# Modulation vectors of a two-layer diffusion transformer: two chunks of columns to a PSUM bank, turned by transposes and added up by VectorE

## The chip, the cores and the metric

The kernel runs on one core of a Trainium2 chip. The time is what the device takes for one launch, in microseconds (us); the numbers of the kernel before come from three runs and one profiled execution. Engines are named as in the profile: PE (matrix products; PEld is its weight load), DVE (VectorE), ACT (ScalarE), POOL (GpSimd) and SP (here only a queue of DMA issues). PEclk is the clock that PE was granted, as a share of full speed.

## The reference

Everything is fp32. Two layers work on 512 tokens and 256 context tokens of width 1024. For each layer two vectors, `c` for the tokens and `c_ctx` for the context, give six modulation vectors of 1024 each:

```python
mod = silu(c) @ mod_w[l] + mod_b[l]          # 6 x 1024 columns, and the same for c_ctx
sh1, sc1, g1, sh2, sc2, g2 = split(mod, 6)
h = rmsnorm(x, ln1) * (1 + sc1) + sh1
x = x + g1 * (mixer(h) @ w_out)
h = rmsnorm(x, ln2) * (1 + sc2) + sh2
x = x + g2 * moe(h)
```

The mixer of layer 0 is dense attention (8 heads on 2 key heads) beside a convolution module; that of layer 1 is attention in a window, with the context and a sink, beside a pooling mixer. `moe` routes each token to 2 experts of 32.

## The kernel before

**Modulation.** `mod_w` comes in chunks of 512 columns, 12 a layer, four pages of 512 KB each (`load`, L126 to 131). `silu_c` holds silu(c) and silu(c_ctx) as two columns of a block of 32, the other 30 zero. `gemv` (L183 to 202) multiplies a chunk in eight products: four column groups of PE take a row block each, so a bank of PSUM has four partial sums in partitions 0, 32, 64 and 96 (and the next ones, for c_ctx), and a second round adds to them (L189). DVE copies the bank (L193). `finish`, which is called later, turns rows into columns and adds the four partial sums in one go: four products with the selection matrix `s2` (L198), each 128 columns of rows against 128x2. DVE adds the bias `mod_bT` from PSUM into `modT` (L199). PE executes an fp32 product as several records, so the trace shows 16 records for the eight products and 8 for the four selections. `gemv_first` (L204 to 222) does the same for the first four chunks of layer 0, in which a chunk holds 256 columns of the shift and 256 of the scale; it lies between the norms of the first tokens. Two more chunks are computed between the projections (`mixer_ab_in`).

**Who uses the columns.** `mod_rows` (L233 to 241) transposes eight column blocks, copies them (`grow`) and stores them to DRAM as a row, from where `row_bcast` (L256) reads it into all partitions: g1, A2 and B2 in the output projection. `router_bias` (L245 to 253) takes the second norm's shift through the router.

**Layer 0's attention** (`mixer_ab_att`) works on 24 units, a pair of heads and a tile of 128 queries each; three are in flight. In each step i PE does the scores of unit i (L482), the transposes of unit i-1's probabilities (L522) and the values of unit i-2 (L537); DVE takes the maxima (L493) and sums, ACT the exponentials (L500) and the copies of transposes (L530) and outputs (L450). `extra(i)` is called at the end of a step, `between(i)` in its middle; they carry the other work, among it taps of the convolution on DVE and POOL (L749, L760). Chunks 6 to 11 of layer 0 and 0 to 3 of layer 1 are computed in `extra` of i = 0, 2 ... 18, and each is finished in the next step. The stores of rows follow chunk 9.

**Layer 1's attention** (`mixer_cd_att`) has 16 units of the same kind. The remaining eight chunks of layer 1 are computed in i = 0 to 7; the weights w_out of the output projection are loaded in i = 4 and 5 and split into a rounded part (ACT, L290, `high`) and a rest (DVE, L295, `low`) one page a step in i = 6 to 13, the rest always in the next step's `between`. `low` gives the page's place back.

**Places and order.** All weights lie in a list of places of 4 KB a partition. A new tile takes the first place of the list, and its load or write waits till the last user of that place is done. The experts' loads (`ahead`, L1326 to 1335) are issued by SP as far as there are places in the list. Each engine keeps the program's order, but for PE, DVE and POOL in two stretches (layer 0's output projection and layer 1's attention), in which the compiler puts first what it holds to be ready. SP issues in the program's order within a stretch: at the start of layer 1's output projection these are 14 loads of experts' pages and then the load of `g1b`, the first gate in all partitions, which `OutProj` multiplies with the products of w_out (L626, L634), before X is updated (L635) and transposed for the second norm (L645).

```python
            if 0 <= n < len(jobs):
                fin.append(gemv(*jobs[n], mods.pop(0)))
                if todo:
                    mods.append(load(a["mod_w"][1, todo.pop(0)]))
                if n in (4, 5):
                    raw.append(load(a["w_out"][1, n - 4]))
```

Of the kernel before, what the change touches and what calls it, by code (L numbers as in the profile page):

```python
# [7 lines left out]
F32 = mybir.dt.float32  # L8
# [4 lines left out]
OP = mybir.AluOpType  # L13
# [26 lines left out]
# engines that do not keep the program's order, by region: 3 is the first layer's output projection, 6 the second's attention  # L40
FREE = {3: [PE, mybir.EngineType.DVE, POOL], 6: [PE, mybir.EngineType.DVE, POOL]}
# pages of the experts' first weights that a layer loads ahead: before the gate, and then at three points of its start
G1 = 3
FIRST = ((11, 0, 2), (7, 3, 2))
# pages beside the lasting ones that a layer's experts have: from the output projection on, and from the experts on
NT = (9, 11)
NS = (9, 3)
# chunks of the second layer's modulation: the tiles at which two are loaded, and how many the attention begins with
M1 = (4, 5)
M2 = 2  # L50
# the row block of the output projection after which the pages that were free before it are taken
# [17 lines left out]
def hybrid_dit_kernel(ctx: ExitStack, tc: tile.TileContext, a, out):  # L69
# [7 lines left out]
    def by_hand(r):  # L77
        """All engines but those given keep the program's order; those take what is ready first."""
        engines = set(ENGINES) - set(FREE.get(r, ()))
        if engines != held[-1]:  # L80
            held.append(engines)
            sched.close()
            sched.enter_context(tc.manual_schedule(engines=engines))
# [13 lines left out]
    class Pages:  # L97
        """Places of 4 KB a partition for weights and other data, each held by one tile after another: what is rounded
        for TensorE's one-pass products and what is not are tiles of their own."""
# [26 lines left out]
    def load(src, n=4, pools=None, queue=nc.sync):  # L126
        """The first n pages of a chunk of weights"""
# [33 lines left out]
    silu_c = keep.tile([128, KT, 32], F32, name="silu_c")  # L161
    modT = keep.tile([128, 2, 48, 2], F32, name="modT")

    def warm(func):
        """Has ScalarE load the function's table ahead of its use"""
# [15 lines left out]
    roomy = []  # L181

    def gemv(l, ch, w):  # L183
        """Products of a chunk of 512 columns; four column groups of the array take a row block each."""
        ps = sm("mps")
        for i in range(2):
            for g in range(4):
                k = 4 * i + g
                nc.tensor.matmul(ps[g * 32:(g + 1) * 32, :], silu_c[:, k, :], w[k // 2][:, k % 2 * 512:(k % 2 + 1) * 512],  # L189
                                 start=(i == 0), stop=(i == 1))  # L190
        pages.done(w)
# [3 lines left out]
        def finish():  # L195
            pt = sm("mpt")
            for b in range(4):
                nc.tensor.matmul(pt[:, 2 * b:2 * b + 2], rows[:, b * 128:(b + 1) * 128], C("s2"), start=True, stop=True)  # L198
            nc.vector.tensor_tensor(modT[:, l, ch * 4:ch * 4 + 4, :], pt[:, 0:8].rearrange("p (b r) -> p b r", r=2),  # L199
                                    mbT[:, l, ch * 4:ch * 4 + 4, None].to_broadcast([128, 4, 2]), OP.add)  # L200
        return finish

    def gemv_first(n, w):
        """The shift and the scale of a pair of row blocks in layer 0's first norm"""  # L204
        ps = sm("mps")
        for c in range(2):
            for i in range(2):
                for g in range(4):
                    nc.tensor.matmul(ps[g * 32:(g + 1) * 32, c * 256:(c + 1) * 256], silu_c[:, 4 * i + g, :],
# [5 lines left out]
        def finish():  # L215
            pt = sm("mpt")
            for b in range(4):
                nc.tensor.matmul(pt[:, 2 * b:2 * b + 2], rows[:, b * 128:(b + 1) * 128], C("s2"), start=True, stop=True)
            dst, b = (m[:, 0, 0:16].rearrange("p (c k) r -> p c k r", c=2)[:, :, 2 * n:2 * n + 2] for m in (modT, mbT[:, :, :, None]))
            nc.vector.tensor_tensor(dst, pt[:, 0:8].rearrange("p (c k r) -> p c k r", c=2, r=2),  # L220
# [1948 lines left out]
```

## Time and profile before

| | |
|---|---|
| runs | 1768.14, 1769.58 and 1769.0 us, median 1769.0 |
| profiled execution | 1769.0 us, the span of its profile |
| instructions | 24713 |
| PE busy | 1567.2 us, 89%; mean granted clock 0.966 |
| DVE busy | 913.2 us, 52% |
| ACT, POOL busy | 528.4 us (30%), 427.4 us (24%) |
| DMA | 519.03 MB, mean 293 GB/s |
| stages | start to 58 us, projections of layer 0 to 187, its attention to 331, its experts to about 990, layer 1's attention 1069 to 1180, its output projection to 1220, its experts to the end |

A row of the timeline gives the start, the duration, the engine, the line of the kernel, the output and inputs by the program's names and the shapes; equal instructions in a row are put together with their count, and their duration is from the first one's start to the last one's end. In brackets stands how long the engine was idle before, and whose end released it. The queue of an engine's DMA issues is named with a q (SPq).

### The profile page before, as it was taken

What the parts mean: (1) busy time and instruction counts of PE and PEld (TensorE: products, weight loads), DVE (VectorE), ACT (ScalarE), POOL (GpSimd) and SP (SyncE); (2) the same over time, 40 slices, a digit from 0 to 9 for tenths busy, and PEclk for the clock granted to TensorE, in tenths of its full rate; (3) what the DMA queues carried; (4) which work ended last, traced back from release to release, by engine and by line L of the source; (5) the groups of instructions that cost most, each with busy time, mean ns of one, the idle gap of its engine ahead of it and who ended that gap; (6) DMA issues with size and microseconds to landing.
All of it is one profiled execution on the core that took longest, in us unless ns stands there. A gap on an engine that the chain in (4) does not pass through costs nothing. (4 is left out here: it accounts for less than half of the span.)

```text
span 1769.0 us, 24713 instructions
## 1 busy us (share of the span) xinstructions
PE 1567.2 (89%) x8732; PEld 866.9 (49%) x8732; DVE 913.2 (52%) x1747; ACT 528.4 (30%) x1036; POOL 427.4 (24%) x347
## 2 busy tenths in 40 slices
PE   5979689997899999998986789989799999989997
PEld 4867457885333333332321676677334344343442
DVE  3897889788333232322333656656534445344454
ACT  3422468733111111111112434663312122121221
POOL 1535556132112112211111223201121121111110
PEclk9999799999999999999999899999799999999999
DMA  9121743447999999999998338145699999999992
GB/s 368 58 83 66 292 155 122 164 148 278 354 396 397 388 390 386 391 394 389 392 400 332 123 108 319 58 180 188 257 408 408 408 408 406 408 406 406 405 407 91
DMA packets 151597, 519.03 MB, mean 293 GB/s; under 512 B 22445, under 2 KB 23181, under 8 KB 151437
## 3 DMA queue, kind: packets, MB, share of 16 engines
q1 hardware_dynamic: 134300, 479.67, 69.2%
q0 software_dynamic: 11520, 16.81, 3.7%
q10 hardware_dynamic: 5616, 20.45, 3.0%
q8 instruction: 97, 1.59, 0.4%
q14 instruction: 64, 0.52, 0.1%
HBM read 510.49 MB, written 21.02 MB: 300 GB/s over the span
## 5 line engine op out<-in xcount | busy, mean ns | idle before, releaser
L1476 PE MATMUL gu<-w,xt 128*64 128x512 f32 x2304 | 516.7, 597 | 21.1 <-DMA w<-in_ex_dram 11.9
L1476 PEld LDWEIGHTS gu<-w,xt 128*64 128x64 f32 x2304 | 171.5, 137 | 326.6 <-issue 247.6
L1500 PE MATMUL yy<-w,ht 128*64 128x512 f32 x1152 | 264.8, 601 | 14.2 <-PEq L1296 5.9
L1482 DVE TENSOR_TENSOR hh<-hh,gu 128x512 f32<-128x512 f32 x64 | 44.1, 688 | 451.6 <-ACT hh L1481 451.6
L1481 ACT ACTIVATE hh<-gu 128x512 f32<-128x512 f32 x64 | 38.3, 598 | 566.2 <-PEq L1296 416.2
L1500 PEld LDWEIGHTS yy<-w,ht 128*64 128x64 f32 x1152 | 81.4, 137 | 172.4 <-issue 133.7
L1379 POOL DMA_INDIRECT xD<-ys,sidx x40 | 70.6, 1765 | 317.8 <-DVE ys L1375 315.3
L1409 POOL TENSOR_TENSOR lo<-ys,hi 64x1024 fp32r<-64x1024 f32 x29 | 68.2, 2351 | 325.0 <-ACTq L1296 325.0
L749 DVE SCALAR_TENSOR_TENSOR acc<-glu,convp,acc 128x784 f32<-128x784 f32 x76 | 97.9, 1288 | 1.6
L760 POOL TENSOR_TENSOR part<-part,prod 128x784 f32<-128x784 f32 x40 | 84.7, 2118 | 43.2 <-ACT prod L759 42.2
L1375 DVE TENSOR_TENSOR ys<-yy,ys 128x512 f32<-128x512 f32 x64 | 44.3, 692 | 97.8 <-PEq L1296 53.4
L1408 ACT ACTIVATE hi<-ys 64x1024 fp32r<-64x1024 f32 (+1 forms) x35 | 34.4, 983 | 193.1 <-DVE ys L1386 108.8
L1352 POOL DMA_INDIRECT Xg<-hD,gidx x40 | 42.6, 1066 | 188.9 <-PE xtp L1460 179.7
L264 POOL TENSOR_TENSOR rs<-ms,mhalf 128x1 f32<-128x1 f32 (+2 forms) x40 | 41.5, 1038 | 170.8 <-DVE ms L262 170.3
L1390 DVE TENSOR_TENSOR X<-X,cmb 128x512 f32<-128x512 f32 x126 | 77.0, 683 | 1.6 <-PE cmb L1426 1.1
L1426 PE MATMUL cmb<-hi,oh 128*128 128x512 f32 x128 | 58.0, 453 | 22.2 <-DVE oh L1413 20.5
L1460 PEld LDWEIGHTS xtp<-cst,Xg 128*128 128x128 f32 x512 | 58.0, 146 | 34.6 <-PEq L1296 18.6
L1460 PE MATMUL xtp<-cst,Xg 128*128 128x128 f32 x512 | 64.8, 282 | 9.1 <-PEq L1296 9.1
L522 PE MATMUL ptp<-cst,P 128*128 128x128 f32 x368 | 53.3, 284 | 18.7 <-POOL P L510 10.5
L1494 DVE COPY ht<-htp 128x512 f32<-128x512 f32 x64 | 43.8, 684 | 50.0 <-PE htp L1489 50.0
L695 PE MATMUL qps<-wh,hi 128*128 128x256 f32 (+1 forms) x176 | 61.4, 349 | 8.0 <-DVE hi L1819 2.4
L687 DVE TENSOR_SCALAR xt<-xtp,A,modT 128x128 f32<-128x128 f32 x128 | 49.6, 410 | 35.7 <-ACT xt L689 34.6
(310 smaller groups left out, 2633.9 us busy)
## 6 DMA issues: line engine op xcount, KB each, us to landing
w<-in_ex_dram SPq DMA_DIRECT2D x751, 512.0 KB
w<-in_mod_w_dram SPq DMA_DIRECT2D x96, 512.0 KB
w<-in_ex_dram ACTq DMA_DIRECT2D x17, 512.0 KB
w<-in_w_out_dram SPq DMA_DIRECT2D x16, 512.0 KB
w<-in_w_in_ab_dram SPq DMA_DIRECT2D x14, 512.0 KB
hD<-x ACTq DMA_DIRECT2D x8, 512.0 KB
xD<-X ACTq DMA_DIRECT2D x6, 512.0 KB
w<-in_w_in_cd_dram ACTq DMA_DIRECT2D x6, 512.0 KB
```

The lines of the kernel that those rows point to most:

```text
L522: nc.tensor.transpose(ps[:, (c - c0) * 128:(c - c0 + 1) * 128], u["P"][c // nk][:, c % nk * 128:(c % nk + 1) * 128], ident)
L687: nc.vector.tensor_scalar(dst[:, k, :], src, g, b, op0=OP.mult, op1=OP.add)
L695: nc.tensor.matmul(ps[:, o:o + n], h(x, k, tk), w(p, k, 0, n), start=(k == 0 and c == 0), stop=(k == KT - 1 and c == 2))
L749: nc.vector.scalar_tensor_tensor(acc, glu[:, ct, i:i + CW], w(i), acc, OP.mult, OP.add)
L760: nc.gpsimd.tensor_tensor(self.part[ct], self.part[ct], t, OP.add)
L1379: return nc.gpsimd.indirect_dma_start(out=xD[:, :], out_offset=bass.IndirectOffsetOnAxis(ap=idx, axis=0), in_=ys[:, :], in_offset=None, bo ...
L1390: nc.vector.tensor_tensor(x, x, ps, OP.add)
L1409: eng.tensor_tensor(lo[rows, c], ys[rows, c], hi[rows, c].bitcast(F32), OP.subtract)
L1426: nc.tensor.matmul(ps, oh[:, tok(t)], y[:, c * 512:(c + 1) * 512], start=(i == 0), stop=(i == 1))
L1460: nc.tensor.transpose(ps[:, k * 128:(k + 1) * 128], src[:, (h * 4 + k) * 128:(h * 4 + k + 1) * 128], ident)
L1476: nc.tensor.matmul(self.gu[c * 64:(c + 1) * 64, b, :], xt[:, k, q * 64:(q + 1) * 64], w[k][:, c * 512:(c + 1) * 512], start=(k == 0), stop ...
L1500: nc.tensor.matmul(yy[c * 64:(c + 1) * 64], t[:, b, f % 2, f // 2, :], w[f][:, c * 512:(c + 1) * 512], start=(f == 0), stop=(f == 3))
```

## The change

`silu_c` gets 34 columns a block, with the two vectors in columns 2 and 3, so that a window of 32 columns that begins at 2 has them in rows 0 and 1 of the product, and one that begins at 0 in rows 2 and 3. `gemv` takes one chunk or two: the second one's products are added to the same bank with the other window, and their rows land beside the first one's. One copy takes both. In `finish` four transposes (`over_partitions`) bring the 512 columns over the partitions, and DVE adds the four partial sums by a reduction for each chunk, and then the bias to both. `gemv_first` and the two chunks in the projections use the same transposes and reductions on single banks. In the attention of both layers the chunks go in pairs, at other steps; the loads of w_out, their splitting and the stores of rows move with them in layer 1, and the stores of rows in layer 0.

```diff
-    silu_c = keep.tile([128, KT, 32], F32, name="silu_c")
+    silu_c = keep.tile([128, KT, 34], F32, name="silu_c")
...
+    def over_partitions(rows):
+        pt = sm("mpt")
+        for b in range(4):
+            nc.tensor.transpose(pt[:, b * 128:(b + 1) * 128], rows[:, b * 128:(b + 1) * 128], ident)
+        return pt.rearrange("p (b g s) -> p b s g", b=4, g=4)
...
-    def gemv(l, ch, w):
+    def gemv(l, ch, ws):
         ps = sm("mps")
-        for i in range(2):
-            for g in range(4):
-                k = 4 * i + g
-                nc.tensor.matmul(ps[g * 32:(g + 1) * 32, :], silu_c[:, k, :], w[k // 2][:, k % 2 * 512:(k % 2 + 1) * 512],
-                                 start=(i == 0), stop=(i == 1))
-        pages.done(w)
+        for j, w in enumerate(ws):
+            for i in range(2):
+                for g in range(4):
+                    k = 4 * i + g
+                    nc.tensor.matmul(ps[g * 32:(g + 1) * 32, :], silu_c[:, k, 2 - 2 * j:34 - 2 * j],
+                                     w[k // 2][:, k % 2 * 512:(k % 2 + 1) * 512],
+                                     start=(i == 0 and j == 0), stop=(i == 1 and j == len(ws) - 1))
+            pages.done(w)
...
         def finish():
-            pt = sm("mpt")
-            for b in range(4):
-                nc.tensor.matmul(pt[:, 2 * b:2 * b + 2], rows[:, b * 128:(b + 1) * 128], C("s2"), start=True, stop=True)
-            nc.vector.tensor_tensor(modT[:, l, ch * 4:ch * 4 + 4, :], pt[:, 0:8].rearrange("p (b r) -> p b r", r=2),
-                                    mbT[:, l, ch * 4:ch * 4 + 4, None].to_broadcast([128, 4, 2]), OP.add)
+            pt = over_partitions(rows)
+            cols = slice(ch * 4, (ch + len(ws)) * 4)
+            for j in range(len(ws)):
+                c = (ch + j) * 4
+                nc.vector.tensor_reduce(modT[:, l, c:c + 4, :], pt[:, :, 2 * j:2 * j + 2, :], AX.X, OP.add)
+            nc.vector.tensor_tensor(modT[:, l, cols, :], modT[:, l, cols, :],
+                                    mbT[:, l, cols, None].to_broadcast([128, 4 * len(ws), 2]), OP.add)
...
-            pt = sm("mpt")
-            for b in range(4):
-                nc.tensor.matmul(pt[:, 2 * b:2 * b + 2], rows[:, b * 128:(b + 1) * 128], C("s2"), start=True, stop=True)
+            pt = over_partitions(rows)
...
-            nc.vector.tensor_tensor(dst, pt[:, 0:8].rearrange("p (c k r) -> p c k r", c=2, r=2),
-                                    b.to_broadcast([128, 2, 2, 2]), OP.add)
+            for c in range(2):
+                nc.vector.tensor_reduce(dst[:, c], pt[:, 2 * c:2 * c + 2, 0:2, :], AX.X, OP.add)
+            nc.vector.tensor_tensor(dst, dst, b.to_broadcast([128, 2, 2, 2]), OP.add)
...
-            n = i // 2
-            if i % 2 == 0 and n < len(jobs):
-                fin.append(gemv(*jobs[n], mods.pop(0)))
-                if n + 2 < len(jobs):
-                    mods.append(load(a["mod_w"][jobs[n + 2][0], jobs[n + 2][1]]))
+            n = i // 2 - 1
+            if i % 4 == 2 and n < len(jobs):
+                fin.append(gemv(*jobs[n], [mods.pop(0), mods.pop(0)]))
+                for nx in jobs[n + 2:n + 4]:
+                    mods.append(load(a["mod_w"][nx]))
+                if n == 2:
+                    fin.append(rows)
                 if n == 4:
-                    fin.append(rows)
-                if n == 6:
                     fin.append(lambda: mod_rows(0, "g2", modT[:, 0, 40:48, :]))
-                if n >= len(jobs) - 2:
-                    hh = n - len(jobs) + 2
-                    wo[hh] = Split(raw[hh], 512)
-                    st.extend((wo[hh], t) for t in raw[hh])
+            if i in (16, 18):
+                hh = i // 2 - 8
+                wo[hh] = Split(raw[hh], 512)
+                st.extend((wo[hh], t) for t in raw[hh])
...
-            if 0 <= n < len(jobs):
-                fin.append(gemv(*jobs[n], mods.pop(0)))
-                if todo:
-                    mods.append(load(a["mod_w"][1, todo.pop(0)]))
-                if n in (4, 5):
-                    raw.append(load(a["w_out"][1, n - 4]))
+            n = 2 * (i // 3)
+            if i % 3 == 1 and n < len(jobs):
+                fin.append(gemv(*jobs[n], [mods.pop(0), mods.pop(0)]))
+                for _ in range(2):
+                    if todo:
+                        mods.append(load(a["mod_w"][1, todo.pop(0)]))
+                if n == 4:
+                    raw.extend(load(a["w_out"][1, c]) for c in range(2))
+                    fin.append(rows)
                 if n == 6:
-                    fin.append(rows)
-                if n == 7:
                     fin.append(lambda: mod_rows(1, "g2", modT[:, 1, 40:48, :]))
-                if n >= len(jobs) - 2:
-                    hh = n - len(jobs) + 2
-                    wo[hh] = Split(raw[hh], 512)
-                    st.extend((wo[hh], t) for t in raw[hh])
+                    for hh in range(2):
+                        wo[hh] = Split(raw[hh], 512)
+                        st.extend((wo[hh], t) for t in raw[hh])
```

The two windows of `silu_c` are set by the activation that now writes columns 2 and 3 instead of 0 and 1.

## Rows read from the trace of the kernel before

**Rows 1.** Table of stretches: us, busy us (instructions) by engine, PE's granted clock, DMA share, GB/s.

```profile
15.00:58.00 43.00, 40.08 (x299) 29.41 (x300) 18.59 (x36) 14.51 (x21) 9.65 (x13) 1.00 0.73 283
187.00:262.00 75.00, 52.88 (x379) 33.30 (x380) 61.67 (x111) 42.46 (x96) 40.97 (x29) 0.82 0.56 217
262.00:331.00 69.00, 68.94 (x681) 56.13 (x679) 62.71 (x93) 59.05 (x116) 31.74 (x24) 1.00 0.29 106
1069.00:1134.00 65.00, 60.13 (x525) 40.58 (x524) 43.67 (x121) 34.17 (x89) 21.44 (x20) 0.95 0.65 256
1134.00:1167.00 33.00, 27.94 (x261) 22.67 (x261) 25.84 (x69) 28.49 (x73) 5.62 (x6) 1.00 0.11 36
1180.00:1220.00 40.00, 39.67 (x207) 32.58 (x206) 21.39 (x67) 9.15 (x20) 2.90 (x9) 1.00 0.29 112
1260.00:1740.00 480.00, 441.39 (x2067) 193.93 (x2062) 209.10 (x378) 100.54 (x182) 81.32 (x42) 1.00 1.00 394
```

**Rows 2.** Groups by line, 150 to 420 us: count, busy us, mean ns, idle before.

```profile
L193 DVE COPY mrows<-mps 128x512 f32<-128x512 f32 x12 | 8.2, 682 | 4.7 <-PE mps L189 4.7
...
L199 DVE TENSOR_TENSOR modT<-mpt,mbT 128x8 f32<-128x8 f32 x12 | 1.8, 152 | 0.5 <-PE mpt L198 0.5
...
L1162 DVE TENSOR_REDUCE m<-em 128x1 f32<-128x32 f32 x8 | 1.5, 187 | 0.3
```

**Rows 3.** PE's timeline, from 162: start, duration, instruction, count, [idle before <- releaser].

```profile
162.09 0.95 PE L198 MATMUL mpt<-cst,mrows 128*128 128x2 f32 x8
162.91 1.07 PE L400 MATMUL qtp<-cst,W 128*128 128x128 f32 x8
163.81 0.60 PE L404 MATMUL ktp<-cst,ks 128*128 128x128 f32 x4
```

**Rows 4.** PE's timeline at the start: the first chunk's selection products.

```profile
20.63 1.87 PE L218 MATMUL mpt<-cst,mrows 128*128 128x2 f32 x8 [0.81 <-DVE mrows L213]
```

**Rows 5.** DVE's timeline, first half of layer 0's attention.

```profile
199.98 0.69 DVE L193 COPY mrows<-mps 128x512 f32<-128x512 f32 x1 [1.73 <-PE mps L189]
...
257.34 0.28 DVE L239 COPY grow<-gps 16x128 f32<-16x128 f32 x1 [2.55 <-DMA rowA<-grow]
```

**Rows 6.** PE's timeline, second half of layer 0's attention.

```profile
289.96 1.66 PE L482 MATMUL S<-low,hi 128*128 128x512 f32 x8
...
294.32 1.92 PE L189 MATMUL mps<-w,silu_c 128*32 128x512 f32 x16
296.18 1.66 PE L482 MATMUL S<-low,hi 128*128 128x512 f32 x8
```

**Rows 7.** PE's timeline, first half of layer 0's attention.

```profile
195.54 0.77 PE L482 MATMUL S<-low,hi 128*128 128x256 f32 x2 [8.66 <-DVE room L353]
196.24 3.64 PE L189 MATMUL mps<-w,silu_c 128*32 128x512 f32 x16
```

**Rows 8.** SP's timeline: the loads at the end of layer 1's attention.

```profile
1156.22 0.33 SPq L1333 DMA_DIRECT2D w<-in_ex_dram  x1
...
1167.16 1.31 SPq L1333 DMA_DIRECT2D w<-in_ex_dram  x3
...
1173.97 4.86 SPq L1333 DMA_DIRECT2D w<-in_ex_dram  x7
...
1178.89 0.48 SPq L256 DMA_DIRECT2D g1b<-rowg  x1
```

**Rows 9.** Timelines of DVE and PE at layer 1's output projection.

```profile
1188.89 0.69 DVE L634 TENSOR_TENSOR otmp<-ops,g1b 128x512 f32<-128x512 f32 x1 [12.31 <-DMA g1b<-rowg]
...
1191.78 0.63 PE L645 MATMUL h2p<-cst,X 128*128 128x128 f32 x4 [0.33 <-DVE X L635]
```

**Rows 10.** Timelines of ACT and DVE, last units of layer 1's attention.

```profile
1162.98 1.06 ACT L290 ACTIVATE wh<-w 128x1024 fp32r<-128x1024 f32 x1
...
1176.07 0.28 ACT L450 ACTIVATE oT<-o 128x128 f32<-128x128 f32 x1
...
1164.16 1.23 DVE L295 TENSOR_TENSOR wl<-w,wh 128x1024 fp32r<-128x1024 f32 x1
```

## What the change should do to the time

> **What bounds the kernel now.** I read five views: the table of stretches, to see which engine is full where a chunk of the modulation is computed; the groups by line, for the price of each removed and added instruction; then the timelines of PE, DVE and SP, for what follows what. In the table [rows 1] look for the engine whose busy time fills the stretch. At the start (15 to 58 us) PE is busy 40.08 of 43 us: every PE instruction less counts. In the first half of layer 0's attention (187 to 262) it is DVE, 61.67 of 75 us, and PE ran at a mean clock of 0.82. In its second half (262 to 331) PE has 68.94 of 69 us, but DVE has 62.71 too. In layer 1's attention the units with a chunk (1069 to 1134) are PE's (60.13 of 65), and the units after them (1134 to 1167) nobody's: PE 27.94 of 33. Layer 1's output projection (1180 to 1220) is PE again, 39.67 of 40. From there the experts are bound by the loads of their weights (DMA share 1.00, 394 GB/s), so that what is won or lost before them reaches the end undiminished.
>
> **Prices.** Of a chunk the change removes four selection products, and for every second chunk a copy; per pair it adds four transposes, two reductions and one addition, where two additions stood. On PE a set of selections stands for 0.82 us before the next group (162.09 to 162.91), and the eight transposes behind it for 0.90 (162.91 to 163.81), so four are 0.45 [rows 3]. In the first of the chunks the selections' row lasts 1.87 instead of 0.95 [rows 3, 4], TensorE at half its clock: by that ratio they stand for 1.6 there and four transposes for 0.9. On DVE the copy is 0.68 and the addition from PSUM 0.152; a reduction of 32 elements a partition gives 0.187, and a bare pass over PSUM 0.152 [rows 2]. No row has a reduction of 8x4 strided PSUM elements: between these two, 0.15 to 0.19, I take 0.18. A pair thus costs PE 0.82 x 2 - 0.45 = 1.2 us less and DVE 0.68 + 2 x 0.15 - 2 x 0.18 - 0.15 = 0.4 us less. The products of a chunk (1.86 us, 294.32 to 296.18) [rows 6] stay; two chunks' worth now come in one block.
>
> **Start.** Four first chunks: one at half clock gives 0.7, three give 0.82 - 0.45 = 0.37 each on a full PE, together **-1.8**; PE's wait of 0.81 for DVE's copy ahead of the first set [rows 4] stays. The added reductions lie beside PE's transposes of the tokens, which other engines evacuate. In the projections behind it two single chunks remain single: the one at 162.09 stands in a gap-free PE and gives 0.4, the other none; DVE pays 0.1: **-0.3**.
>
> **Layer 0's attention.** Before, ten chunks are computed in units 0, 2 ... 18; after, five pairs in units 2, 6, 10, 14, 18. Up to unit 10 DVE sets the pace. It is spared three copies (2.0) and two waits for a chunk's products (two rows like the one of 1.73) [rows 5]. Against that, DVE's copy in unit 6 has to wait for twice the products: at half clock one chunk took 3.64 us instead of 1.92 [rows 7], so that the wait can be anything from 0.7 to 4. The vectors for the second norm (line 233) go from unit 9 to unit 7: DVE stands still there for about 2.5 us twice, and the first copy waits again for the row before it to be stored [rows 5]. The stall moves and does not go; what it covered of a chunk in unit 8 is no longer covered in unit 10. I put this half at -1 (-3 to +3). In the second half a unit with a chunk lasts 6.2 us (289.96 to 296.18) and one without 4.4 by taking off the products [rows 6]; DVE needs 5 to 6 in each unit that the convolution is still in. A unit with a pair needs 4.4 + 1.86 x 2 = 8.1 of PE, and the units freed of a chunk fall only as far as DVE lets them: 62.71 of 69 leaves 6 us at most over 15 units. If PE alone counted, three pairs would give 3.2; if the freed units stay at DVE's length, each of the two late pairs costs about 2. I take +1.5. Sum **+0.5** (-4 to +4). The chunks' loads are issued two at a time and are far ahead of their use in both layers, so they cost nothing; the cover is the slack of DMA in these stretches (share 0.56 and 0.29) [rows 1].
>
> **Layer 1's attention.** Before, eight chunks in units 0 to 7; after, pairs in units 1, 4, 7, 10. Nine units with chunks take 65 us, 7.2 each; the rest 33 us, about 5.2 each. There PE works 27.94 us in some 6.3 units, 4.4 in each, so a unit is 5.2 us of chain however little PE has. The four pair units cost 4.4 + 3.7 = 8.1, the others 5.2 to 5.5 with what transposes are left: against 98 before about 94: **-4** (-7 to -1) at the end of the last unit's scores.
>
> **What waits instead.** Splitting w_out into its two parts (lines 286 to 308) moves in layer 1 from units 6 to 13 to units 10 to 17, one page a unit. A split frees the page's place, and the first 14 loads of layer 1's experts wait for such places on SP, in the order written. Before, they trickle out from 1156.22 on; three go at 1167.16, when the last scores are done, and the last seven from 1173.97, at 4.86 / 7 = 0.69 us each; right behind them, at 1178.89, comes the load of g1b, the first gate's row in all partitions [rows 8]. DVE waits 12.31 us for it, till 1188.89, and PE then 0.33 us for X [rows 9]: before, g1b has no slack at all. Following the list of free places through the changed program, the first of the 14 now gets the place that the last unit's scores free, the next three those of the last three w_out pages, and ten more and g1b stand behind. The last page's split comes behind the last copy of outputs, 1176.07 + 0.28, by a high part of 1.06 and a low part of 1.23 [rows 10]: 1178.6, that is 11.5 after the last scores. From there twelve transfers of 524,288 B (the fourth page, ten more, g1b) at 394 GB/s, 1.33 us each, end at 27.5; before, g1b came at 21.7 after the same point. That is 5.8 later as the least, since it counts nothing between a load's issue and its first bytes; by the issues (ten by 0.69 and then the 10.0 that the load took before) it is 6.7, and with the larger backlog behind it up to 8.8. I take 7.5. The Trainium skill, "DMA: Bandwidth & Descriptors", section "Where 436 GB/s comes from", says that the HBM side holds a core to about 358 GB/s; as an estimate by that page a load is 1.46 us, twelve are 1.6 us longer and the time is 1775.0. The trace does not agree: the experts' stretch moves 394 GB/s for 480 us [rows 1].
>
> PE's products of the first two tiles run on till X is wanted and then stop: 7.5 - 4 = **+3.5** later than before. And a PE that stood still starts slowly: after 8.66 us without work a chunk's products took 3.64 instead of 1.92 [rows 7], and all the work till the clock was back about 2.5 more; a stop of 7 us is of that size: **+2.5** (0 to 2.7). Layer 0's loads wait for the same release as before and are left out.
>
> Sum: -1.8 - 0.3 + 0.5 + 3.5 + 2.5 = +4.4. The profiled execution's span is 1769.0 us, and so are its own time and the median of the runs: 1773.4.
>
> **Rivals.** *Faster: PE is not held by g1b.* If X's gate arrives in time (its load gets ahead of the pages, or the places come free in another order), layer 1's 4 us pass on: -1.8 - 0.3 + 0.5 - 4 = -5.6, 1763.4; decided where g1b is late by less than the attention gains. For it: the gain of every part on PE is sure. Against it: SP's order is written and g1b is already the last to come [rows 8, 9]. 0.28, with 0.02 more for a PE that gains all 1.2 us of all nine pairs (near 1757). *No change: late, but little.* With g1b at its least (+5.8 - 4 = 1.8) and no loss of clock the sum is -1.8 - 0.3 + 0.5 + 1.8 = +0.2, near 1769; 1766 to 1772 with layer 0 by 3 us either way. 0.25. *Slower by more: the doubled blocks.* In layer 0 DVE waits at half clock for two chunks in units 6 and 10, and PE's long units 14 and 18 are not evened out: +4 there, and 1776.9. 0.07.
>
> **How the numbers follow.** About 0.2% (3.5 us) is what a measurement of this kernel can tell from no change. The forecast has 0.38; with the last rival slower is 0.45, the same 0.25, faster 0.30. The time is that of the forecast. The range goes from 1762.0, a little below the first rival, to 1779.0, the forecast with layer 0 at +4 and the gate 1.3 later, its bound (1778.2), and rounded up; it leaves out the lower part of the first rival (layer 0 at -1 or less) and the tail above. The forecast alone is 1770 to 1779.
>
> **What would show it.** In the changed kernel's timelines: PE gap-free and some 2 us ahead at 58; the last scores of layer 1 about 5.6 us earlier; SP's first expert load only behind them; g1b's load issued near 1180 and DVE waiting for it till about 1190; before the h2p transposes PE idle for some 7 us, with a granted clock below 1.00 behind it. I am wrong if g1b's wait ends before PE has run out of products, or if layer 0's attention is shorter by more than 4 us.

## The result, and the profile after

The changed kernel takes 1778.0 us (median; 1775.75 to 1781.69), 9.2 us more than before (1768.8, 1768.14 to 1769.58): a ratio of 1.0052, interval 1.0037 to 1.0066. Timed again beside other kernels it gave 1777.8, ratio 1.0052 (1.0035 to 1.0069). It is slower by 0.5%, the forecast was 0.25%. Ratios are to the kernel before, timed again beside each group. Single executions of one kernel lie up to 6 us either side of its median, so below a time is a median of 4 to 12 runs, and what happened inside is read as a distance between two places of the same trace. One of the ten runs of l0_single (below) took 3991.85 us and does not count in its ratio; without it the median there is 1771.6 instead of 1772.0. The profiled execution after has a span of 1774.1 us against 1769.0.

**Where the time went.** The starts of the same instructions in both traces (in us, from the timelines of PE; the first scores come in two halves, since the second needs a tile that DVE prepares):

| place | before | after | later by |
|---|---|---|---|
| first scores of layer 0, first half | 186.40 | 184.34 | -2.06 |
| the same, second half | 195.54 | 195.72 | +0.18 |
| last scores of layer 0 | 326.51 | 329.57 | +3.06 |
| first scores of layer 1 | 1069.48 | 1071.02 | +1.54 |
| last scores of layer 1 (its last product) | 1166.97 | 1162.99 | -3.98 |
| first h2p transposes of layer 1 | 1190.86 | 1194.33 | +3.47 |
| last products of w_out, layer 1 | 1228.78 | 1234.91 | +6.13 |

So 5.1 us are lost from the first scores of layer 0 to its last, layer 1's attention gains 5.5, and between its last scores and the end of the output projection 10.1 are lost. How far such distances repeat can be seen in before_g1_first (below), where the edit lies behind both attentions: layer 0's attention, from the second half of its first scores to its last, takes 129.2 us there and 131.0 in the trace of the kernel before, layer 1's 95.8 and 97.5. The changed kernel's traces agree better, 133.9 and 133.6, 92.0 and 92.5. The table of stretches of the changed kernel, to be held against [rows 1], with two stretches more around the h2p transposes:

```profile
15.00:58.00 43.00, 39.42 (x291) 28.75 (x292) 20.18 (x45) 15.63 (x24) 9.93 (x14) 1.00 0.72 283
185.00:260.00 75.00, 50.33 (x337) 33.95 (x341) 64.79 (x111) 42.42 (x96) 41.61 (x29) 0.73 0.56 210
260.00:331.00 71.00, 67.32 (x633) 52.58 (x626) 60.17 (x94) 57.06 (x114) 33.09 (x23) 0.98 0.25 97
1071.00:1136.00 65.00, 56.43 (x518) 40.23 (x518) 45.17 (x140) 40.47 (x110) 20.34 (x22) 0.97 0.68 256
1136.00:1163.00 27.00, 24.49 (x219) 17.80 (x216) 17.27 (x47) 19.39 (x48) 4.72 (x5) 0.94 0.00 1
...
1180.00:1195.00 15.00, 5.34 (x25) 4.15 (x23) 2.17 (x4) 1.25 (x3) 0.00 (x0) 0.72 0.77 311
1195.00:1235.00 40.00, 39.76 (x208) 32.64 (x208) 23.97 (x85) 11.43 (x25) 3.44 (x10) 0.93 0.32 112
1260.00:1740.00 480.00, 441.20 (x2068) 193.28 (x2066) 209.29 (x384) 101.95 (x186) 81.26 (x42) 1.00 1.00 397
```

Three things are to be seen. In the first half of layer 0's attention DVE is busier than before (64.79 of 75, was 61.67), though it has half the copies, and PE's granted clock is 0.73 instead of 0.82. In the second half PE is no longer full: 67.32 of 71, was 68.94 of 69. And from 1180 to 1195 PE works 5.34 of 15 us, where it had no gap before.

**That gap** is g1b's. SP's timeline after, answering to [rows 8]:

```profile
1163.21 0.33 SPq L1344 DMA_DIRECT2D w<-in_ex_dram  x1
...
1169.46 0.33 SPq L1344 DMA_DIRECT2D w<-in_ex_dram  x1
...
1172.23 8.03 SPq L1344 DMA_DIRECT2D w<-in_ex_dram  x11
...
1182.50 0.33 SPq L267 DMA_DIRECT2D g1b<-rowg  x1
```

and the timelines of DVE and PE, answering to [rows 9]:

```profile
1192.76 0.69 DVE L645 TENSOR_TENSOR otmp<-ops,g1b 128x512 f32<-128x512 f32 x1 [17.82 <-DMA g1b<-rowg]
...
1194.33 1.08 PE L656 MATMUL h2p<-cst,X 128*128 128x128 f32 x4 [9.66 <-DVE X L646]
```

The first expert load no longer goes before the last scores (1156.22 before) but right behind them (1163.21), the second six us later, the rest when the last pages of w_out have been split; g1b goes behind all of them, 19.5 us after the last scores instead of 11.9, and lands 29.8 after them instead of 21.9. PE runs out of products 9.66 us before X is there.

**Layer 0** has the other losses. DVE's timeline after, where the two single chunks of the projections are finished, and GpSimd's at the same times:

```profile
165.37 1.64 DVE L211 TENSOR_TENSOR modT<-modT,mbT 128x8 f32<-128x8 f32 x1
...
189.22 0.18 DVE L210 TENSOR_REDUCE modT<-mpt 128x8 f32<-128x32 f32 x1
189.44 1.59 DVE L211 TENSOR_TENSOR modT<-modT,mbT 128x8 f32<-128x8 f32 x1
```

```profile
164.52 2.46 POOL L771 TENSOR_TENSOR part<-part,prod 128x784 f32<-128x784 f32 x1 [3.50 <-ACT prod L770]
...
188.59 2.41 POOL L771 TENSOR_TENSOR part<-part,prod 128x784 f32<-128x784 f32 x1 [3.50 <-ACT prod L770]
```

An addition of eight numbers a partition takes 1.64 and 1.59 us: it ends at 167.01 and 191.03, when GpSimd's instruction ends (166.98 and 191.00). That of before read PSUM and took 0.152 [rows 2]. Not all of it is lost, for before a small instruction a little further on lasted till GpSimd's end, and now it does not. Here it is before, and then after:

```profile
190.89 0.89 DVE L262 TENSOR_SCALAR ms<-qss 128x10 f32<-128x10 f32 x1
```

```profile
191.79 0.17 DVE L273 TENSOR_SCALAR ms<-qss 128x10 f32<-128x10 f32 x1
```

So each of the two finishes costs DVE 0.9 us: it leads the kernel before by 1.70 us ahead of the first, by 0.75 behind it, and is 0.18 late behind the second (starts of L353 before and L364 after, 159.92 and 158.22, 171.50 and 170.75, 194.57 and 194.75). The last of these prepares the first scores' second half, so PE's wait there grows (8.66 before, [rows 7]):

```profile
195.72 0.77 PE L493 MATMUL S<-low,hi 128*128 128x256 f32 x2 [10.90 <-DVE room L364]
```

Of these 2.24 us, 1.88 are DVE's loss, and 0.36 are what PE itself had gained in the projections.

Further on, PE's timeline has two waits in `mod_rows`:

```profile
239.49 0.37 PE L248 MATMUL gps<-cst,A 128*16 128x128 f32 x1 [3.31 <-DVE A L239]
...
268.13 0.27 PE L248 MATMUL gps<-cst,modT 128*16 128x128 f32 x1 [1.80 <-DVE modT L211]
```

and the table of stretches around the second of them:

```profile
265.00:268.00 3.00, 1.33 (x18) 0.91 (x14) 2.87 (x8) 3.00 (x8) 0.25 (x1) 1.00 0.54 220
268.00:274.00 6.00, 5.87 (x45) 5.32 (x45) 4.44 (x6) 3.42 (x8) 4.36 (x3) 0.72 0.49 172
```

The rows of the second norm, and those of the second gate, are transposed right behind the finish of the very pair that they need; before, they came two steps later. PE keeps the order in layer 0, so it stands and waits for DVE, and after the second wait its granted clock is 0.72 over 6 us. The first of the two waits was there before too, at about half the length:

```profile
251.89 0.27 PE L237 MATMUL gps<-cst,A 128*16 128x128 f32 x1 [1.70 <-DVE A L228]
```

### The profile page after: what moved, and what is told of

Same layout as the page of the kernel before. It is cut to its first block, busy times and chain, and to the rows that moved or that the text cites. A ratio compares the mean times of both kernels' runs of the same rounds, so it can differ in the third digit from the quotient of the medians.

```text
span 1774.1 us, 24468 instructions
## 1 busy us (share of the span) xinstructions
PE 1557.8 (88%) x8600; PEld 859.0 (48%) x8600; DVE 914.6 (52%) x1757; ACT 527.2 (30%) x1036; POOL 426.6 (24%) x347
## 5 line engine op out<-in xcount | busy, mean ns | idle before, releaser
L1390 POOL DMA_INDIRECT xD<-ys,sidx x40 | 71.1, 1778 | 316.9 <-DVE ys L1386 314.4
L1471 PEld LDWEIGHTS xtp<-cst,Xg 128*128 128x128 f32 x512 | 58.2, 145 | 34.8 <-PEq L1307 18.8
L541 ACT ACTIVATE pT<-ptp 128x512 f32<-128x512 f32 (+1 forms) x96 | 53.6, 593 | 49.9 <-PE ptp L533 49.8
```

The source lines that it names most:

```text
L541: nc.scalar.activation(dst, src, AF.Copy)
L1390: return nc.gpsimd.indirect_dma_start(out=xD[:, :], out_offset=bass.IndirectOffsetOnAxis(ap=idx, axis=0), in_=ys[:, :], in_offset=None, bo ...
L1471: nc.tensor.transpose(ps[:, k * 128:(k + 1) * 128], src[:, (h * 4 + k) * 128:(h * 4 + k + 1) * 128], ident)
```

## The experiments

Lines in the diffs are those of the changed kernel. Beside the times the distance from layer 1's last scores to its last products of w_out is given, 61.8 us before and 71.9 after.

**g1_first.** `OutProj` takes g1b from its caller, who loads it before `more()` issues the expert loads:

```diff
-            slot = more()
             with pool_of("m1c") as work:
+                g1 = work.tile([128, D], F32, name="g1b")
+                row_bcast(1, "g1", 0, g1)
+                slot = more()
```

> The changed kernel with one edit: in layer 1 the load of g1b goes ahead of the experts' first 14 loads on SP. Theory (g1b's place behind the pages costs the time): DVE's wait for g1b falls from 17.8 us to under 12, PE's idle time before the h2p transposes from 9.66 us to under 1, PE's granted clock in the output projection is 1.00, and the time falls by the 7.5 + 2.7 us that lay between the last scores and the end of the projection: 1767 to 1770. Rival (the late splitting of w_out holds PE, and g1b only comes at the same time): PE still stops for 5 us or more ahead of h2p or in the products of w_out, and the time stays at 1775 to 1779.

Measured: 1763.9 us, ratio 0.9968 to before (0.9954 to 0.9983), so 14 us less than the changed kernel, even faster than before, and 3 below the 1767 to 1770 that were expected. SP's timeline and the stretch that had the gap:

```profile
1163.30 0.33 SPq L267 DMA_DIRECT2D g1b<-rowg  x1
1163.72 19.24 SPq L1344 DMA_DIRECT2D w<-in_ex_dram  x14
```

```profile
1180.00:1195.00 15.00, 15.00 (x79) 12.61 (x78) 8.94 (x28) 5.58 (x13) 1.29 (x4) 1.00 0.78 315
```

PE is full at a clock of 1.00 and stands neither for g1b nor for X ahead of the first h2p transposes; the distance is 59.0 us, 12.9 less. The rival falls: the late splits alone do not hold PE.

**split_two.** g1b stays behind the pages, but w_out is split two pages a step, from step 10 to 13:

```diff
-            if st:
-                w, t = st.pop(0)
-                w.high(t)
-                low.append(lambda: w.low(t))
+            for w, t in [st.pop(0) for _ in range(min(2, len(st)))]:
+                w.high(t)
+                low.append(lambda w=w, t=t: w.low(t))
```

> The changed kernel with one edit: in layer 1 two pages of w_out are split in each step from 10 on, so that the last is split in step 13 instead of 17; g1b stays behind the 14 expert loads. Theory (g1b is late because those loads wait for the places that the splits free): three of the first four loads go before the last scores, g1b's load is issued at least 4 us sooner after them, and PE's stop before the h2p transposes falls from 9.7 us to under 3; 1768 to 1772. Rival (it is the number of pages ahead of g1b alone): the stop stays above 6 us, 1775 to 1778.

Measured: 1769.5 us (1.0010, 0.9998 to 1.0022), distance 61.3 us. SP's timeline:

```profile
1153.39 20.63 SPq L1344 DMA_DIRECT2D w<-in_ex_dram  x14
1174.06 0.62 SPq L267 DMA_DIRECT2D g1b<-rowg  x1
```

The loads start 9.6 us before the last scores again, g1b goes 11.1 us after them, and PE does not stop. Layer 1's attention takes 95.3 us here, 3.3 more than in the changed kernel, which g1_first does not pay (92.7). So the two ends of the chain are both shown: g1b is late because it stands behind 14 loads, and those are late because they wait for places that the moved splits give back.

**before_g1_first.** The same edit as in g1_first, in the kernel before.

> The kernel before, with the load of g1b ahead of the experts' first loads. PE waited only 0.33 us for X there, so by the theory this edit is worth nothing to it: 1767 to 1770. Rival (g1b and the pages share the DMA engines for longer than the waits show, so that the edit is a gain of its own): 1761 to 1765, and then what g1b first gains in the changed kernel is not the cost of the change.

Measured: 1768.3 us (1.0003, 0.9993 to 1.0013). g1b's place was worth nothing before; the 10.1 us behind the last scores are the change's. In all traces the distance agrees with this: 71.8 to 72.0 us where w_out is split late and g1b stands last (the changed kernel twice, l0_single, late_rows), 59.0 to 61.8 in all others.

**l1_single.** Layer 1's attention goes back to single chunks in steps 0 to 7, with w_out's loads and splits where they were:

```diff
-            n = 2 * (i // 3)
-            if i % 3 == 1 and n < len(jobs):
-                fin.append(gemv(*jobs[n], [mods.pop(0), mods.pop(0)]))
...
+            n = i
+            if 0 <= n < len(jobs):
+                fin.append(gemv(*jobs[n], [mods.pop(0)]))
...
```

> The changed kernel with layer 1's attention back at the order of before: eight single chunks at steps 0 to 7, with transposes and reductions; w_out's loads and splits at their old steps. Theory (g1b is late because the splits are): the last scores come 4 to 5.5 us later than in the changed kernel, the first expert loads trickle out before them again, DVE waits 12 us for g1b and PE less than 1 us; 1778 + 5 - 10 = 1773. Rival (the stop of PE has another cause, so that only the attention's gain is lost): 1781 to 1784.

Measured: 1765.9 us (0.9986, 0.9973 to 0.9999), below both expectations. PE's wait is gone as the theory has it (the waits of PE from 1160 to 1200 us: us in total, times, longest):

```profile
PE h2p L656 <- DVE X L646: 0.4, 1, 0.4
```

and the distance is 60.5. What failed is the price of the attention: from first to last scores it takes 93.6 us, against 92.0 in the changed kernel and 97.5 before. I had taken the whole gain of 5.5 for the pairs'; with single chunks 1.6 of it is lost, so most of it comes with the cheaper finish. That accounts for 3.4 of the 7 us by which the theory was too high.

**l0_single.** Layer 0's attention goes back to single chunks in steps 0 to 18, rows and splits where they were:

```diff
-            n = i // 2 - 1
-            if i % 4 == 2 and n < len(jobs):
-                fin.append(gemv(*jobs[n], [mods.pop(0), mods.pop(0)]))
...
+            n = i // 2
+            if i % 2 == 0 and n < len(jobs):
+                fin.append(gemv(*jobs[n], [mods.pop(0)]))
...
```

> The changed kernel with layer 0's attention back at the order of before: ten single chunks at steps 0, 2 ... 18, each with its copy, four transposes, one reduction and one addition; the row stores and splits of w_out at their old steps. Theory (the pairs are what costs layer 0's attention 5 us): the last scores of layer 0 come 3 to 5 us earlier than in the changed kernel, and the time is 1773 to 1775. Rival (transposes, reductions and the addition in SBUF cost it, whatever the steps): the last scores come within 1 us of the changed kernel's or later, 1777 to 1780.

Measured: 1772.0 us (1.0011, 0.9999 to 1.0024), 6 less than the changed kernel and 1 below what the theory gave. From the second half of the first scores to the last scores the attention takes 129.0 us; in the changed kernel 133.9 (133.6 in its other execution), before 131.0 (129.2 in before_g1_first). In all traces it is 132.8 to 133.9 us with pairs and the rows where the change has them, and 129.0 to 129.9 with single chunks. A difference of the same size is to be seen in one group of DVE's, the taps of the convolution from 184 to 330 us. In the changed kernel

```profile
L760 DVE SCALAR_TENSOR_TENSOR acc<-glu,convp,acc 128x784 f32<-128x784 f32 x25 | 36.4, 1455 | 0.3
```

and here

```profile
L760 DVE SCALAR_TENSOR_TENSOR acc<-glu,convp,acc 128x784 f32<-128x784 f32 x25 | 31.5, 1262 | 0.3
```

The same 25 instructions, 1455 ns each with pairs and 1262 with single chunks (1314 before). The shortest of them take 1.01 to 1.03 us, one beside GpSimd's instructions 2.41. The five copies that the pairs save (3.4 us) are paid back here. That the 4.9 us of taps are the cause, and not a sign of units that fall less well beside GpSimd's work, was not tried, and late_rows below speaks against taking the one for the other.

**both_single.** Both edits together; of the change remain the transposes, reductions and additions.

> Both attentions back at the order of before; what is left of the change is transposes, reductions and additions in place of the selection products, at the start, in the projections and in 18 single chunks. Theory (the pairs and what moves with them cost the time, the transposes themselves save a little PE and cost a little DVE): 1766 to 1770, within 0.2% of before. Rival (the new finish of a chunk is itself dearer, by DVE's additions in SBUF beside GpSimd): 1772 to 1776.

Measured: 1766.7 us (0.9986, 0.9967 to 1.0004). The new finish is not dearer, the rival falls. The attentions take 129.4 and 94.0 us, against 131.0 and 97.5 before and 129.2 and 95.8 in before_g1_first. So in layer 1 the new finish gains 2 to 3.5 us here (1 to 4 with the 93.6 and 94.8 of the other two kernels with single chunks there); in layer 0 no gain is shown.

**after_again.** Unchanged, since l0_single and l1_single did not add up.

> The changed kernel once more, as it is, beside the others of this group: single executions of one kernel have been seen 5 us apart, and layer 0's pairs were worth 6.0 us with layer 1's pairs (1778.0 against 1772.0) but -0.8 with layer 1's single chunks (1765.9 against 1766.7). If the two parts are independent, the mean of these, some 2.6 us, is all, and the changed kernel is nearer to 1775; if they really add to each other it is 1778 again.

Measured: 1777.8 us. The sum that does not add up is real as far as these intervals go: taking layer 0's pairs out is worth 5.8 us beside layer 1's pairs, nothing (-0.8) without them.

**l0_single_g1_first.** Single chunks in layer 0, pairs in layer 1, and g1b first.

> Layer 0's attention in the order of before with single chunks, layer 1's in pairs, and the load of g1b ahead of the experts' pages. Theory (layer 0's pairs cost up to 4 us at the last scores, of which part is absorbed before layer 1; g1b's place costs about 10): 1758 to 1762, faster than both kernels. Rival (what layer 0 loses is absorbed in its experts, whose loads set their time): 1763 to 1765, the same as with pairs and g1b first (1763.9).

Measured: 1759.2 us, ratio 0.9954 (0.9937 to 0.9971): faster than both kernels, 18.8 us below the changed one. Against g1_first (0.9954 to 0.9983) the intervals overlap, so that this is the best of the variants is not settled.

**late_rows.** The pairs stay, the two sets of rows go two steps later:

```diff
-                if n == 2:
-                    fin.append(rows)
-                if n == 4:
-                    fin.append(lambda: mod_rows(0, "g2", modT[:, 0, 40:48, :]))
+            if i == 8:
+                fin.append(rows)
+            if i == 12:
+                fin.append(lambda: mod_rows(0, "g2", modT[:, 0, 40:48, :]))
```

> The changed kernel with one edit in layer 0's attention: the vectors of the second norm go to rows in step 9 instead of 7 and the second gate in step 13 instead of 11, so no longer right behind the finish of the pair that they need. Theory (PE, which keeps the order, stops for DVE's additions there, 3.31 and 1.80 us, and runs on at a lower clock): the wait for the second gate's columns is gone, the granted clock after it is 1.00, layer 0's last scores come 2 to 4 us earlier than in the changed kernel, and the time is 1774 to 1776. Rival (the long blocks of products of a pair cost it, and DVE beside them): the last scores come within 1 us, 1777 to 1779.

Measured: 1773.0 us (1.0033, 1.0022 to 1.0045). The wait of 1.80 is gone, and the stretch that ran at 0.72 now reads

```profile
268.00:274.00 6.00, 4.79 (x50) 3.86 (x48) 5.96 (x7) 4.98 (x12) 5.26 (x4) 1.00 0.34 137
```

The other wait stays, though its columns are ready two steps earlier:

```profile
248.50 0.27 PE L248 MATMUL gps<-cst,A 128*16 128x128 f32 x1 [3.01 <-DVE A L239]
```

It is for the gain that `rows` itself has DVE compute just ahead, behind whatever DVE is at. From the second half of the first scores the attention takes 131.8 us, 2 of the 5 lost ones come back. DVE's taps still take 35.6 us, 0.8 less, so the taps' length and the attention's do not go together one for one. The time is 1 below what the theory gave, and its interval overlaps the changed kernel's.

**late_rows_g1_first.** The same with g1b first.

> The same edit with the load of g1b ahead of the experts' pages, to be held against the pairs with g1b first (1763.9) and against single chunks in layer 0 with g1b first (1759.2). Theory (the rows are what makes the pairs dearer): 1759 to 1762. Rival (the pairs themselves are): 1763 to 1765.

Measured: 1764.4 us (0.9970, 0.9958 to 0.9983), the same as g1_first; here the rival's number came, although this trace has the shorter attention too (132.6). So the late rows help layer 0's attention by 1 to 2 us, and whether that reaches the end isn't shown: one pair of runs says 4.8, the other nothing.

**best_add_psum.** In l0_single_g1_first the reductions write to another PSUM bank, from which the addition reads:

```diff
-                nc.vector.tensor_reduce(modT[:, l, c:c + 4, :], pt[:, :, 2 * j:2 * j + 2, :], AX.X, OP.add)
-            nc.vector.tensor_tensor(modT[:, l, cols, :], modT[:, l, cols, :],
+                nc.vector.tensor_reduce(p2[:, j * 8:j * 8 + 8].rearrange("p (b r) -> p b r", r=2), pt[:, :, 2 * j:2 * j + 2, :], AX.X, OP.add)
+            nc.vector.tensor_tensor(modT[:, l, cols, :], p2[:, 0:8 * len(ws)].rearrange("p (b r) -> p b r", r=2),
```

> Single chunks in layer 0, pairs in layer 1 and g1b first (1759.2), and the reductions of a chunk write to PSUM, so that the addition of the bias reads its first operand there instead of in SBUF. Theory (the addition with both operands in SBUF is held up while GpSimd works, 1.59 us at the worst where others take 0.16): the additions of layer 0's attention fall from 296 ns to some 155 in the mean, the second half of the first scores in layer 0 comes 1 us earlier after the first, and the time falls by 0 to 2 us. Rival (the length has another cause): the additions stay at 250 ns or more.

Measured: 1766.8 us (0.9991, 0.9980 to 1.0003), 7.6 more. The additions do what the theory says (the group of DVE's, 184 to 330 us; 296 ns without the edit):

```profile
L211 DVE TENSOR_TENSOR modT<-mq,mbT 128x8 f32<-128x8 f32 x11 | 1.8, 167 | 0.4
```

Most of that mean is the one long addition at the second finish in the projections; those in the attention took 0.17 us already. And DVE's loss in the projections is gone: between the two places used above (L364 at 158 us and ahead of the first scores) lie 34.70 us, as before (34.65), where the changed kernel has 36.53 and l0_single_g1_first 36.50. This shows that the operand in SBUF was the cause of that loss. But PE waits 1.1 us for the new tile `mq` ahead of the first scores and 2.6 us for `modT` ahead of layer 1's `mod_rows`, waits that l0_single_g1_first does not have, and layer 1's attention grows from 94.3 to 97.9 us. The edit takes one tile more from a ring of four PSUM banks; that this is why was not tried, and these marks do not account for all of the 7.6.

**both_single_g1_first.** Single chunks in both layers and g1b first.

> Single chunks in both attentions in the order of before, with transposes and reductions, and the load of g1b ahead of the experts' pages; to be held against pairs in layer 1 (1759.2) and against the same without that edit (1766.7). Theory (layer 1's attention gains by the transposes, 97.5 to 94.0 us, and hardly more by the pairs; and with the splits early g1b's place is worth nothing, as in the kernel before): the last scores of layer 1 are 94 us after the first, PE's wait for X ahead of the transposes is under 1 us, and the time is 1764 to 1767; the best version then owes its lead to the late splits giving the loads of experts back their turn. Rival (single chunks are as good as pairs once g1b is first): 1758 to 1761.

Measured: 1765.0 us (0.9988, 0.9975 to 1.0000), as the theory has it. So with g1b first the pairs of layer 1 are worth 5.8 us, with intervals that don't overlap. The traces do not say where: in the two profiled executions the attention takes 94.3 us with pairs and 94.8 without, and the distance is 59.0 and 59.8. Those two executions took 1763.8 and 1762.7 us, the other way round than the medians, so they can't show it.

## Why the prediction was right, and where it was not

The sign and the mechanism were right, the size was half. By its own steps:

| step | predicted | measured in the profiled execution |
|---|---|---|
| start | -1.8 | -1.7 (first `glu` on DVE, 57.60 instead of 59.29) |
| projections | -0.3 | +1.9 up to the second half of the first scores |
| layer 0's attention | +0.5 (-4 to +4) | +2.9 from there to the last scores |
| from there to layer 1's first scores | 0 | -1.5 (see below) |
| layer 1's attention | -4 (-7 to -1) | -5.5 |
| g1b after the last scores | +7.5 (5.8 to 8.8) | 29.8 - 21.9 = +7.9, of which 7.5 reach the h2p transposes |
| clock behind PE's stop | +2.5 (0 to 2.7) | from +3.47 to +6.13: +2.7 |
| sum at the end of the projection | +4.4 | +6.1 |

Held against before_g1_first's attentions (129.2 and 95.8) the two would read +4.7 and -3.9: they are known to 2 us. Of the signs that were named, layer 1's last scores came 4.0 us earlier and not 5.6, since layer 0 had lost more.

**The wait that takes the place of the work** was read from the trace of before: g1b without slack, the loads ahead of it bound to places, the splits moved behind the last scores. Forecast were a load of g1b issued 18.4 us after the last scores, landing at 21.7 + 7.5 = 29.2, and a stop of PE of some 7 us; measured were 19.5, 29.8 and 9.66. The three experiments on it (g1_first, split_two, before_g1_first) leave it no rival: 12.9 us of distance go with one reordered load. The rival "faster: PE is not held by g1b" is what g1_first makes of the change, and its number is met (1763.9 where it said 1763.4), but partly by luck: in that trace layer 0's last scores are 1.8 us later than before, where the rival had them 1.6 earlier, and the distance behind layer 1's is 2.8 shorter than before, which the rival did not count.

**The step that failed is "DVE pays 0.1"** in the projections. I priced DVE's additions by the row of one that read PSUM; the new one has both operands in SBUF, and two of them lasted till GpSimd's instruction ended. They cost DVE 1.9 us (best_add_psum shows it). Costing the projections' PE gain as if PE set the pace there was the second half of the mistake: the first scores wait for DVE (8.66 us before, 10.90 after), so the 0.36 that PE gained only made it wait longer.

**The +0.5 for layer 0's attention** was too small, by 2.4 us here and by 4.2 against before_g1_first. The additions are not the reason, since in the attention they took 0.17 to 0.41 us. What is shown is that the pairs go with it (l0_single) and that the place of the rows is a part of it (late_rows, 2 us); that taps of the convolution last longer is seen beside it, and why stays open.

**Two readings in the working** were off without weight for the sum. The last price is 0.68 + 0.30 - 0.36 - 0.15 = 0.47, not 0.4. And that TensorE ran at half its clock in the first chunk is read from the length of a row alone (1.87 instead of 0.95): the granted clock on record for 15 to 58 us is 1.00 [rows 1]. There the selections stood for 1.72 us and the transposes stand for 0.90, a gain of 0.8 where 0.7 was put.

**"The stall moves and does not go"** was right but incomplete: the wait for A went on, 3.31 us instead of 1.70, and a stall beside it was new, PE's wait for additions that the same step had just asked for (1.80 us and a granted clock of 0.72 behind it); late_rows shows it and gets 2 us of attention back.

**"Reaches the end undiminished"** can't be judged in one execution. Of 3.06 us at layer 0's last scores 1.54 are left at layer 1's first, but from the one to the other the kernels with pairs in layer 0 took 739.3 to 744.6 us and those without 740.0 to 744.5: the stretch itself, mostly experts bound by their loads, varies by as much as the whole loss. What layer 0's pairs cost at the end is therefore told by the times alone: 5.8 us with layer 1 as changed, 4.7 with g1b first (intervals overlap), -0.8 with layer 1's single chunks.

Open stays the rest of the 9.2: the end of the projection explains 6.1 and the span 5.1 in this execution, the medians more. The order of the variants is settled by intervals only between the far ones: the changed kernel (1778), with late_rows (1773.0) not told from it; those near before (1764 to 1772); and single chunks in layer 0 with pairs in layer 1 and g1b first (1759.2), which is not told from g1_first and late_rows_g1_first.

## What to carry to other kernels

When work moves later in a stage, look for whatever is released by its end, and for what stands behind that in an in-order queue: here a load of 512 KB that nobody had touched became 7.9 us late, and one reordered line turned a loss of 0.5% into a gain of 0.3%. A small instruction is priced by where its operands lie and who else works there, not by its size. And a step that needs the result of the one before it should not be put right behind it on an engine that keeps its order.

## What the runs showed of the hardware

- A DVE addition of 128x8 numbers took 1.59 us beside a GpSimd instruction, ending with it to 0.03 us, and 0.15 to 0.17 when its first operand lay in PSUM. The Trainium skill, "SBUF — State Buffer", section "SBUF: two separate sides", has this: DVE with two SBUF inputs and a GpSimd instruction that reads SBUF take a shared pair of ports for a whole instruction, and the one that comes second stands still. The trace agrees: 1.59 us, ending at 191.03 and 191.00, and again 0.41 us, ending at 293.51 and 293.49, beside GpSimd instructions that had started 0.85 and 0.52 us earlier. The other four in layer 0's attention, with both operands in SBUF too, began within 0.06 us of a GpSimd instruction's start and took 0.17 to 0.18.
- The profile shows such a wait as busy time of DVE, not as idle, so busy time is no measure of work: the same 25 taps counted 32.8 us busy before, 36.4 with pairs and 31.5 with single chunks.
- A reduction of 128x8 out of 128x32 PSUM elements took 0.17 to 0.18 us, where the prediction had taken 0.18 between bounds of 0.15 and 0.19.
